# Four seven-product pairs per gate and up unit, with two of their sums made by accumulating transfers

## The chip, the core and the metric

One core of a Trainium2 chip runs the kernel. The metric is the time on the device in microseconds (us), the median of several runs. Five engines work side by side, each through its own queue in order: TensorE (PE) multiplies, VectorE (DVE) and ScalarE (ACT) do elementwise work, GpSimd (POOL) and SyncE (SP) here mostly start transfers. Which instruction stands where in each queue is decided when the program is built, by a scheduler of the library that the kernel is written with; the program cannot change that order while it runs.

## The reference

A decoder layer in float32 on 256 tokens with 16 meta tokens ahead: a SwiGLU block, a mixer (differential attention beside a short convolution, gated and merged), a second SwiGLU block and a norm. What the change touches is the second SwiGLU and the gates of the merge:

```python
def swiglu_ffn(h, w_gu, w_down):
    gate, up = jnp.split(h @ w_gu, 2, axis=-1)
    return (jax.nn.silu(gate) * up) @ w_down
...
        z = jnp.einsum('blnw,nwd->blnd', ys, w_branch[layer])
        gates = jax.nn.sigmoid(h @ w_gate[layer]).reshape(Bsz, L, N_BRANCH, D_MODEL)
        merged = jnp.sum(gates * z, axis=2)
        s = s + merged @ w_out[layer]

        h = rms_norm(s, norm_ffn2[layer])
        s = s + 0.5 * swiglu_ffn(h, ffn2_w_gu[layer], ffn2_w_down[layer])
```

`D_MODEL` is 2048 and `D_FF` 5632. By the end of the mixer only the 256 real tokens are carried on.

## The kernel before, in words

**Split products.** Each float32 operand is split into a high and a low part. ACT casts a weight tile to its high part `wh` (L378), DVE subtracts it from the tile and keeps the rest as `wl` (L379); both lie in rings of three tiles (`W_BUFS`). A product of an activation block and a weight block is then three matmuls into one PSUM bank: high by `wh` (L485), low by `wh` (L486), high by `wl` (L487). Each has 128 rows and 512 columns here.

**Units.** `Mixed`, `linear_mix` and `mixed` compute two outputs of 512 columns for 256 tokens at once: a gate and an up group of the second SwiGLU (10 of its 11 groups; the first is done plainly by `linear_tok`), or the two gates of the merge (4 units). One such call is called a unit here. It runs over 8 pairs of 128-row chunks, and `KINDS` says how each pair is multiplied. A "D" pair takes the 2 x 2 x 2 block product as it stands: 8 products, in 2 weight tiles of 4 products each. An "S" pair uses seven products of sums of blocks (a scheme of Strassen's kind): 4 weight tiles with 1, 2, 2 and 2 products. The eight accumulators are called "1" to "7" and "x". `KINDS = "DDDSDSDS"` has three S pairs (3, 5 and 7, counted from 0), so a unit has 5 x 24 + 3 x 21 = 183 matmuls.

**Sums.** The four sums of activation blocks of an S pair are made once (`pair`, kept in tiles `sp`). Its four weight sums are made for each unit from the loaded tile `st`, on DVE, when the pair is loaded, one pair ahead: L512 makes two of them (the first and third) in one instruction of 128x1024, L513 and L514 the other two (128x512 each). The four lie in one tile `tt`, taken from the same ring of five (`ST_BUFS`) as the loads.

**Order.** `parts` splits a tile, and `step` keeps the tile's products back until two further tiles have been split (`AHEAD = 2`). When a product's accumulator is complete, `done` evicts it: "1" by an ACT copy into `cup` (L553), "x" by an ACT copy into `u2x` (L548), the others by DVE additions, of which "2" into `cgate` is the first (L558). In an S pair the accumulators end in the order 3, 1, 2, 6, 4, 5, 7. The result of a unit is activated, turned by PE (`mt_ps`, L591) and split (L595, L596) during pair 2 of the next unit. All weights come through SP's queue (L508 here), two transfers of 512 KB for each pair.

**Around the units.** The second SwiGLU runs in thirds of 4, 4 and 3 groups, each followed by a down projection (`linear_tok`, tile names `pd`). POOL has almost nothing to do: a few small loads at the start and, near the end, two loads of 512 KB for the last norm (`gfin`, L986).

Of the kernel before, what the change touches and what calls it, by code (L numbers as in the profile page):

```python
# [29 lines left out]
LAM_INIT = 0.8 - 0.6 * math.exp(-0.3 * 0)  # L30
KB = 2
W_BUFS = 3
ST_BUFS = 5
LB = 2
N_ACT = 27
EVICT_AT = 1
WARM = 6
WARM_PREP = 5
HOLD = 3
LATER_AT = (4, 6)  # L40
KINDS = "DDDSDSDS"
AHEAD = 2


# [1 line left out]
def decoder_layer(ctx: ExitStack, tc: tile.TileContext, t, out):  # L46
# [2 lines left out]
    const = ctx.enter_context(tc.tile_pool(name="const", bufs=1))  # L49
    wpool = ctx.enter_context(tc.tile_pool(name="w", bufs=W_BUFS))  # L50
    apool = ctx.enter_context(tc.tile_pool(name="a", bufs=N_ACT))
    tmp = ctx.enter_context(tc.tile_pool(name="tmp", bufs=2))
    psum = ctx.enter_context(tc.tile_pool(name="ps", bufs=8, space=bass.MemoryType.PSUM))

# [259 lines left out]
    def linear_tok(ops, chunks, k0, name, evict, side_at=(5, 9, 13), hold=0, after=None):  # L314
# [46 lines left out]
        for b, c in enumerate(chunks):  # L361
# [9 lines left out]
            wh, wl = parts(st[:, b % 2])  # L371
            step(lambda b=b, wh=wh, wl=wl: use(b, wh, wl))

    def parts(src, n=2):
# [3 lines left out]
        nc.scalar.copy(out=wh, in_=src)  # L378
        nc.vector.tensor_sub(wl, src, wh.bitcast(F32))  # L379
        return wh, wl  # L380

    ng = F // GW
# [44 lines left out]
    class Mixed:  # L427

        def __init__(self, norm, g0):
            self.act, self.sums = Act("hn", 0, SEQ), {}
            self.norm, self.g0 = norm, g0

        def renorm(self, p):
# [10 lines left out]
        def pair(self, p, f):  # L446

            tl = apool.tile([P, 2, 2, SEQ], F32R, tag="act", name=f"hn{p}")
            self.act.tiles.append(tl)
            nc.scalar.copy(out=tl[:, :, 0, :], in_=f)  # L450
            nc.vector.tensor_sub(tl[:, :, 1, :], f, tl[:, :, 0, :].bitcast(F32))
            if KINDS[p] == "S":
                a11, a12, a21, a22 = (f[:, c, i * P : (i + 1) * P] for i in range(2) for c in range(2))
                q = tmp.tile([P, 4, P], F32, tag="sc", name="sums")
                nc.vector.tensor_sub(q[:, 0, :], a21, a22)
                nc.vector.tensor_sub(q[:, 1, :], q[:, 0, :], a11)
                nc.vector.tensor_sub(q[:, 2, :], a11, a21)
                nc.vector.tensor_add(q[:, 3, :], a12, q[:, 1, :])
                sp = apool.tile([P, 4, 2, P], F32R, tag="act", name=f"sp{p}")
                nc.scalar.copy(out=sp[:, :, 0, :], in_=q)  # L460
                nc.vector.tensor_sub(sp[:, :, 1, :], q, sp[:, :, 0, :].bitcast(F32))
                self.sums[p] = [[sp[:, k, lo, :] for lo in range(2)] for k in range(4)]
# [4 lines left out]
    def linear_mix(a, w, cols, name, done):  # L467

        nd, ns = KINDS.count("D"), KINDS.count("S")
        left = {k: 2 * nd * (k in "234x") + ns * (k != "x") for k in "1234567x"}
        ps = {}

        def product(k, left_op, wh, wl):
            first = k not in ps  # L480
            if first:
                ps[k] = bank(name + k)
            left[k] -= 1
            hi, lo = left_op
            nc.tensor.matmul(ps[k], hi, wh, start=first, stop=False)  # L485
            nc.tensor.matmul(ps[k], lo, wh, start=False, stop=False)  # L486
            nc.tensor.matmul(ps[k], hi, wl, start=False, stop=left[k] == 0)  # L487
            if left[k] == 0:
                done(k, ps[k])

        def use(p, n, products):

            for k, left_op, wh, wl in products:
                product(k, left_op, wh, wl)
            if p == 2 and later:
                later.pop(0)()
            if n == (1 if KINDS[p] == "D" else 3):
                if p == 0:
                    flush()
                if side:  # L500
                    side.pop(0)()

        def load(p):

            st = wpool.tile([P, 2, 2, GW], F32, tag="st", bufs=ST_BUFS, name="st")
            rows = w[2 * p * P : (2 * p + 2) * P, :].rearrange("(c p) f -> p c f", p=P)
            for q in range(2):
                nc.sync.dma_start(out=st[:, :, q, :], in_=rows[:, :, cols[q] : cols[q] + GW])  # L508
            if KINDS[p] == "D":
# [3 lines left out]
            nc.vector.tensor_add(tt[:, 2, :], tt[:, 0, :], st[:, 1, 1, :])  # L513
            nc.vector.tensor_add(tt[:, 3, :], tt[:, 2, :], st[:, 1, 0, :])  # L514
            return st, tt

        loaded = {0: load(0)}
        for p, kind in enumerate(KINDS):
            st, tt = loaded[p]
# [14 lines left out]
            for n, (src, products) in enumerate(tiles):  # L534
                if n == 1 and p + 1 < len(KINDS):
# [5 lines left out]
    def mixed(a, w, cols, name, end):  # L541

        ev = {}

        def done(k, ps):
            if k == "x":
                ev["u"] = wide([P, 2, GW], "u2x")
                nc.scalar.copy(out=ev["u"][:, 1, :], in_=ps)  # L548
            elif k == "3":
                ev["p3"] = ps  # L550
            elif k == "1":
                ev["e"], ev["g"] = wide([P, 2, GW], "cup"), wide([P, 2, GW], "cgate")
                nc.scalar.copy(out=ev["e"][:, 0, :], in_=ps)  # L553
            if k in "x31":
                return
            up, gt, u = ev["e"], ev["g"], ev["u"]
            if k == "2":
                nc.vector.tensor_add(gt[:, 0, :], ps, up[:, 0, :])  # L558
            elif k == "6":
                nc.vector.tensor_add(u[:, 0, :], ps, up[:, 0, :])  # L560
            elif k == "4":
                nc.vector.tensor_add(gt[:, 1, :], ps, u[:, 0, :])
            elif k == "5":
                nc.vector.tensor_sub(up[:, 0, :], ps, u[:, 0, :])
                nc.vector.tensor_add(up[:, 1, :], up[:, 0, :], u[:, 1, :])
                nc.vector.tensor_add(up[:, 0, :], ev["p3"], up[:, 0, :])
            elif k == "7":
                nc.vector.tensor_add(gt[:, 1, :], ps, gt[:, 1, :])
                nc.vector.tensor_sub(up[:, 1, :], up[:, 1, :], ps)

                pending.append(lambda: end(gt, up))

        linear_mix(a, w, cols, name, done)

    def gate_up_mix(a, w_gu, g, m, gi):


        def end(gt, up):
            nc.scalar.activation(gt, gt, AF.Silu)
            nc.vector.tensor_mul(up, up, gt)  # L580
            for k in range(2):
                later.append(lambda k=k: back(m, 2 * gi + k, up, k))

        mixed(a, w_gu, (g * GW, F + g * GW), "pg", end)

    def back(act, g, mt, k):

# [250 lines left out]
    n0 = NMETA - 2  # L838
    nu = T - n0
    yc = Act("yc", NH, SEQ)  # L840
    hg = Mixed(norm2, G_MIX)
# [122 lines left out]
    hn = Mixed(norm3, G_FFN2)  # L964

    def renorm_after(b):
        if b % 2 and b > 1:
# [74 lines left out]
```

## Time and profile before

| What | us |
|---|---|
| median of 3 runs | 2203.83 (2202.94 to 2204.87) |
| the profiled execution, its own time | 2203.69 |
| its span, from the first to the last instruction | 2201.9 |
| granted TensorE clock, share of full speed | 0.999 |
| the four gate units with their branch products, from | 1117 to about 1375 |
| second SwiGLU, plain group, from about | 1475 to 1521 |
| second SwiGLU, ten units and three down projections | 1521 to about 2190 |

The page gives, for each engine, its busy time, then the costliest groups of instructions with the mean time of one and what ended the idle time before them. A view of windows gives the busy time of each engine between two moments; a timeline gives single instructions with their start, their length and, in brackets, how long the engine sat idle before and what released it. Matmuls are pipelined, so the record of one (0.39 us) is longer than the distance to the next; the distance between two starts is what one costs.

### The profile page before, as it was taken

What the parts mean: (1) busy time and instruction counts of PE and PEld (TensorE: products, weight loads), DVE (VectorE), ACT (ScalarE), POOL (GpSimd) and SP (SyncE); (2) the same over time, 40 slices, a digit from 0 to 9 for tenths busy, and PEclk for the clock granted to TensorE, in tenths of its full rate; (3) what the DMA queues carried; (4) which work ended last, traced back from release to release, by engine and by line L of the source; (5) the groups of instructions that cost most, each with busy time, mean ns of one, the idle gap of its engine ahead of it and who ended that gap; (6) DMA issues with size and microseconds to landing.
All of it is one profiled execution on the core that took longest, in us unless ns stands there. A gap on an engine that the chain in (4) does not pass through costs nothing.

```text
span 2201.9 us, 33218 instructions
## 1 busy us (share of the span) xinstructions
PE 2186.8 (99%) x13534; PEld 1973.6 (90%) x13534; DVE 1467.6 (67%) x1904; ACT 1041.3 (47%) x1301; POOL 6.4 (0%) x17
## 2 busy tenths in 40 slices
PE   9999999999999999999999999999999999999998
PEld 9999999999999999898988888888888888888886
DVE  7555554445555565667897777678886688856985
ACT  6343433334343443444555455455554455534554
POOL 0000000000000000000000000000000000000000
PEclk9999999999999999999999999999999999999999
DMA  8555555555555555444545666554566566665562
GB/s 273 173 173 173 174 177 178 179 173 173 172 173 176 178 179 176 154 148 140 173 153 192 210 203 217 175 189 147 196 216 207 164 200 202 220 209 182 182 227 96
DMA packets 192393, 401.96 MB, mean 183 GB/s; under 512 B 8692, under 2 KB 8880, under 8 KB 192240
## 3 DMA queue, kind: packets, MB, share of 16 engines
q1 hardware_dynamic: 191232, 397.97, 55.0%
q8 instruction: 105, 1.72, 0.3%
q0 software_dynamic: 544, 1.21, 0.2%
q10 hardware_dynamic: 464, 0.66, 0.1%
q14 instruction: 48, 0.39, 0.1%
HBM read 397.71 MB, written 2.10 MB: 182 GB/s over the span
## 4 chain that ended last, share of the span: by engine, by line
PE 97%; DVE 1%; ACT 1%; DMA 0%; issue 0%; SPq 0%; DVEq 0%; ACTq 0%
PE pg L487 5%; PE pg L485 5%; PE pg L486 5%; PE pu L289 4%; PE pd L289 4%; PE pd L287 4%; PE pu L287 4%; PE pu L288 4%; PE pd L288 4%; PE pg L289 4%; PE pg L287 4%; PE pg L288 4%; PE pd L329 4%; PE pd L327 4%; PE pd L328 4%; PE o L285 3%
## 5 line engine op out<-in xcount | busy, mean ns | idle before, releaser
L276 DVE TENSOR_TENSOR wl<-st,wh 128x1024 fp32r<-128x1024 f32 x392 | 479.2, 1225 | 453.0 <-ACT wh L275 452.5
L275 ACT CAST wh<-st 128x1024 fp32r<-128x1024 f32 x392 | 411.0, 1049 | 609.8 <-PE pd L288 147.0
L378 ACT CAST wh<-st 128x1024 fp32r<-128x1024 f32 (+1 forms) x360 | 358.6, 1003 | 379.6 <-PE pd L328 129.8
L379 DVE TENSOR_TENSOR wl<-st,wh 128x1024 fp32r<-128x1024 f32 (+1 forms) x360 | 415.6, 1161 | 139.4 <-ACT wh L378 138.7
L287 PE MATMUL pg<-h,wh 128*128 128x272 f32 x704 | 203.0, 289 | 0.4 <-ACT wh L275 0.3
L287 PE MATMUL pu<-h,wh 128*128 128x272 f32 x704 | 203.2, 289 | 0.0
L289 PE MATMUL pu<-h,wl 128*128 128x272 f32 x704 | 203.0, 288 | 0.0
L289 PE MATMUL pd<-m,wl 128*128 128x272 f32 x704 | 203.0, 288 | 0.0
L287 PE MATMUL pd<-m,wh 128*128 128x272 f32 x704 | 203.0, 288 | 0.0
L288 PE MATMUL pd<-m,wh 128*128 128x272 f32 x704 | 202.4, 288 | 0.0
L288 PE MATMUL pu<-h,wh 128*128 128x272 f32 x704 | 202.4, 288 | 0.0
L288 PE MATMUL pg<-h,wh 128*128 128x272 f32 x704 | 201.8, 287 | 0.0
L289 PE MATMUL pg<-h,wl 128*128 128x272 f32 x704 | 200.6, 289 | 0.9 <-DVE wl L276 0.9
L485 PE MATMUL pg<-wh,hn 128*128 128x512 f32 x390 | 152.7, 392 | 0.0
L487 PE MATMUL pg<-wl,hn 128*128 128x512 f32 x390 | 151.9, 392 | 0.2 <-DVE wl L379 0.2
L486 PE MATMUL pg<-wh,hn 128*128 128x512 f32 x390 | 152.0, 390 | 0.0
L327 PE MATMUL pd<-wh,m 128*128 128x512 f32 x352 | 137.6, 391 | 0.0
L328 PE MATMUL pd<-wh,m 128*128 128x512 f32 x352 | 137.1, 389 | 0.0
L329 PE MATMUL pd<-wl,m 128*128 128x512 f32 x352 | 137.0, 390 | 0.0
L379 DVE TENSOR_TENSOR wl<-tt,wh 128x1024 fp32r<-128x1024 f32 x84 | 101.3, 1223 | 52.3 <-ACT wh L378 42.4
L287 PEld LDWEIGHTS pg<-h,wh 128*128 128x128 f32 x704 | 132.3, 188 | 1.0 <-ACT wh L275 1.0
L288 PEld LDWEIGHTS pg<-h,wh 128*128 128x128 f32 x704 | 132.8, 189 | 0.0
(303 smaller groups left out, 4728.5 us busy)
## 6 DMA issues: line engine op xcount, KB each, us to landing
st<-in_ffn_w_gu_dram SPq DMA_DIRECT2D x184, 512.0 KB, 4.7
st<-in_ffn_w_down_dram SPq DMA_DIRECT2D x88, 1024.0 KB, 5.2
st<-in_ffn_w_gu_dram SPq DMA_DIRECT2D x84, 1024.0 KB, 5.1
st<-in_w_in_dram SPq DMA_DIRECT2D x48, 1024.0 KB, 5.1
st<-in_w_gate_dram SPq DMA_DIRECT2D x64, 512.0 KB, 4.6
st<-in_w_branch_dram SPq DMA_DIRECT2D x32, 512.0 KB, 5.0
st<-in_w_out_dram SPq DMA_DIRECT2D x16, 1024.0 KB, 5.0
xin<-in_x_dram SPq DMA_DIRECT2D x8, 256.0 KB, 8.5
```

Of the source, the lines that this page charges most:

```text
L275: nc.scalar.copy(out=wh[:, :m, :], in_=sw)
L276: nc.vector.tensor_sub(wl[:, :m, :], sw, wh[:, :m, :].bitcast(F32))
L287: nc.tensor.matmul(a, wh[:, i, f], act.part(c, 0, t0, t1), start=first, stop=False)
L288: nc.tensor.matmul(a, wh[:, i, f], act.part(c, 1, t0, t1), start=False, stop=False)
L289: nc.tensor.matmul(a, wl[:, i, f], act.part(c, 0, t0, t1), start=False, stop=last)
L327: nc.tensor.matmul(ps, hi, wh[:, q, :], start=first, stop=False)
L328: nc.tensor.matmul(ps, lo, wh[:, q, :], start=False, stop=False)
L378: nc.scalar.copy(out=wh, in_=src)
L379: nc.vector.tensor_sub(wl, src, wh.bitcast(F32))
L485: nc.tensor.matmul(ps[k], hi, wh, start=first, stop=False)
L486: nc.tensor.matmul(ps[k], lo, wh, start=False, stop=False)
L487: nc.tensor.matmul(ps[k], hi, wl, start=False, stop=left[k] == 0)
```

## The change

- FFN2's units get their own kinds, `"DDDSSDSS"`: four S pairs (3, 4, 6, 7) and four D pairs, 4 x 24 + 4 x 21 = 180 matmuls in a unit. The gates keep `"DDDSDSDS"`.
- The four weight sums no longer lie in one tile of the load ring. `t13` holds the first and third, `t24` the other two, each 128 x 1024; `t24`, and in the gates `t13` as well, comes from a ring of two tiles called `tt`. The load ring has four tiles instead of five.
- In FFN2, `t13` is made by POOL: one transfer brings two weight blocks from memory, and a second adds two more to them (`accum_op`). Its tiles come from a ring of three, `aux`. Both transfers are asked for up to four pairs ahead. In the gates DVE still makes `t13` when the pair is loaded.
- `t24` is made on DVE by `sum24`, right behind the first split of its own pair, and is held there by `issue_after`.
- The activation ring has 24 tiles instead of 27; the activation sums of the gates lie in `aux` until FFN2 uses it, and those of FFN2 in the activation ring.

```diff
-ST_BUFS = 5
+ST_BUFS = 4
 LB = 2
-N_ACT = 27
+N_ACT = 24
+N_AUX = 3
...
-KINDS = "DDDSDSDS"
+KINDS_GATES = "DDDSDSDS"
+KINDS_FFN2 = "DDDSSDSS"
...
+    aux = ctx.enter_context(tc.tile_pool(name="aux", bufs=N_AUX))
...
         nc.scalar.copy(out=wh, in_=src)
-        nc.vector.tensor_sub(wl, src, wh.bitcast(F32))
+        split_last[0] = nc.vector.tensor_sub(wl, src, wh.bitcast(F32)).ins
...
-                sp = apool.tile([P, 4, 2, P], F32R, tag="act", name=f"sp{p}")
+                sp = (aux if self.in_aux else apool).tile([P, 4, 2, P], F32R, tag="act", name=f"sp{p}")
...
-            if KINDS[p] == "D":
-                return st, None
-            tt = wpool.tile([P, 4, GW], F32, tag="st", bufs=ST_BUFS, name="tt")
-            nc.vector.tensor_add(tt[:, 0:2, :], st[:, 0, :, :], st.rearrange("p c q f -> p q c f")[:, 1, :, :])
-            nc.vector.tensor_add(tt[:, 2, :], tt[:, 0, :], st[:, 1, 1, :])
-            nc.vector.tensor_add(tt[:, 3, :], tt[:, 2, :], st[:, 1, 0, :])
-            return st, tt
+            if kinds[p] == "D":
+                return st, None, None
+            if fetch:
+                t13 = fetched.pop(p)
+            else:
+                t13 = wpool.tile([P, 2, GW], F32, tag="tt", bufs=2, name="t13")
+                nc.vector.tensor_add(t13, st[:, 0, :, :], st.rearrange("p c q f -> p q c f")[:, 1, :, :])
+            return st, t13, wpool.tile([P, 2, GW], F32, tag="tt", bufs=2, name="t24")
+
+        def sum24(st, t13, t24):
+            nc.vector.tensor_add(t24[:, 0, :], t13[:, 0, :], st[:, 1, 1, :])
+            nc.vector.tensor_add(t24[:, 1, :], t24[:, 0, :], st[:, 1, 0, :])
+
+        fetched = {}
+
+        def prefetch(p):
+            t13 = fetched[p] = aux.tile([P, 2, GW], F32, tag="act", name="t13")
+            rows = w[2 * p * P : (2 * p + 2) * P, :].rearrange("(c p) (q f) -> p c q f", p=P, q=2)
+            fs = slice(cols[0], cols[0] + GW)
+            nc.gpsimd.dma_start(out=t13, in_=rows[:, 0, :, fs])
+            nc.gpsimd.dma_start(out=t13, in_=rows[:, :, 1, fs], accum_op=ALU.add)
...
+            if fetch:
+                for k in range(0 if p == 0 else p + 4, min(p + 5, len(kinds))):
+                    if kinds[k] == "S":
+                        prefetch(k)
+            st, t13, t24 = loaded[p]
...
-                    (tt[:, 2:4, :], (("6", s2, 0), ("4", a22, 1))),
-                    (tt[:, 0:2, :], (("5", s1, 0), ("7", s3, 1))),
+                    (t24, (("6", s2, 0), ("4", a22, 1))),
+                    (t13, (("5", s1, 0), ("7", s3, 1))),
...
                 wh, wl = parts(src, src.shape[1])
+                if kind == "S" and n == 0:
+
+                    with tc.issue_after(split_last[0]):
+                        sum24(st, t13, t24)
```

The scheduler also places the rows around the sums anew. Two places of the seventh unit show it. Lines in the changed program are numbered anew: the cast L378 is now L383, the split L379 is L384, the copies L548 and L553 are L577 and L582, the additions L513 and L514 are L526 and L527, L558 is L587 and L596 is L625. Behind each name stands the number of its buffer.

ACT, around pair 7, before. `wh<-tt` are the casts of the third and fourth weight tile of pair 7, `cup<-pg1` is the eviction of accumulator "1".

```order
L378 CAST wh_18087<-st_18070 128x512
L378 CAST wh_18103<-st_18070 128x1024
L378 CAST wh_18121<-tt_18073 128x1024
L548 COPY u2x_18119<-pgx_17847 128x512
L378 CAST wh_18128<-tt_18073 128x1024
L553 COPY cup_18135<-pg1_17971 128x512
L378 CAST wh_18144<-st_18142 128x1024
```

The same place now; `t24_18205` and `t13_18042` are the third and fourth weight tile of pair 7.

```order
L383 CAST wh_18224<-t24_18173 128x1024
L577 COPY u2x_18222<-pgx_17978 128x512
L383 CAST wh_18231<-t13_18003 128x1024
L383 CAST wh_18241<-st_18202 128x512
L383 CAST wh_18253<-st_18202 128x1024
L582 COPY cup_18277<-pg1_18108 128x512
L383 CAST wh_18263<-t24_18205 128x1024
L383 CAST wh_18270<-t13_18042 128x1024
L383 CAST wh_18286<-st_18284 128x1024
```

The eviction of "1", which stood behind both casts of pair 7's sums, now stands ahead of both.

DVE, from pair 4 (a D pair) to the end of pair 5, before. L512 to L514 make the sums of pair 5.

```order
L379 TENSOR_TENSOR wl_17979<-st_17934,wh_17978 128x1024
L512 TENSOR_TENSOR tt_17992<-st_17989 128x1024
L379 TENSOR_TENSOR wl_17997<-st_17934,wh_17996 128x1024
L513 TENSOR_TENSOR tt_17992<-tt_17992,st_17989 128x512
L379 TENSOR_TENSOR wl_18009<-st_17989,wh_18008 128x512
L514 TENSOR_TENSOR tt_17992<-tt_17992,st_17989 128x512
L379 TENSOR_TENSOR wl_18028<-st_17989,wh_18027 128x1024
L379 TENSOR_TENSOR wl_18044<-tt_17992,wh_18043 128x1024
L379 TENSOR_TENSOR wl_18051<-tt_17992,wh_18050 128x1024
```

DVE now, from pair 3 to the end of pair 4, both S pairs. `m4` and `m5` belong to the unit before; `t24_18025` and `t13_17926` are pair 3's, `t24_18073` and `t13_17929` pair 4's.

```order
L625 TENSOR_TENSOR m4_16843<-mt_ps_18063,m4_16843 128x2x256
L384 TENSOR_TENSOR wl_18098<-t24_18025,wh_18097 128x1024
L625 TENSOR_TENSOR m5_16844<-mt_ps_18090,m5_16844 128x2x256
L384 TENSOR_TENSOR wl_18105<-t13_17926,wh_18104 128x1024
L384 TENSOR_TENSOR wl_18116<-st_18070,wh_18115 128x512
L526 TENSOR_TENSOR t24_18073<-t13_17929,st_18070 128x512
L384 TENSOR_TENSOR wl_18132<-st_18070,wh_18131 128x1024
L527 TENSOR_TENSOR t24_18073<-t24_18073,st_18070 128x512
L384 TENSOR_TENSOR wl_18144<-t24_18073,wh_18143 128x1024
L384 TENSOR_TENSOR wl_18151<-t13_17929,wh_18150 128x1024
```

The second half of `t24` now stands behind the split of the pair's second tile, directly ahead of the split that needs it.

More of the change, by code (lines that the diff above doesn't have):

```diff
@@ L372, in linear_tok @@
             step(lambda b=b, wh=wh, wl=wl: use(b, wh, wl))
+    split_last = [None]
     def parts(src, n=2):
@@ L427, in decoder_layer, with __init__ @@
     class Mixed:
-        def __init__(self, norm, g0):
-            self.act, self.sums = Act("hn", 0, SEQ), {}
+        def __init__(self, kinds, norm, g0, in_aux):
+            self.kinds, self.act, self.sums, self.in_aux = kinds, Act("hn", 0, SEQ), {}, in_aux
             self.norm, self.g0 = norm, g0
@@ L451, in pair @@
             nc.vector.tensor_sub(tl[:, :, 1, :], f, tl[:, :, 0, :].bitcast(F32))
-            if KINDS[p] == "S":
+            if self.kinds[p] == "S":
                 a11, a12, a21, a22 = (f[:, c, i * P : (i + 1) * P] for i in range(2) for c in range(2))
@@ L465, in block, with linear_mix @@
             return [self.act.part(c, lo, i * P, (i + 1) * P) for lo in range(2)]
-    def linear_mix(a, w, cols, name, done):
-        nd, ns = KINDS.count("D"), KINDS.count("S")
+    def linear_mix(a, w, cols, name, done, fetch):
+        kinds = a.kinds
+        nd, ns = kinds.count("D"), kinds.count("S")
         left = {k: 2 * nd * (k in "234x") + ns * (k != "x") for k in "1234567x"}
@@ L496, in use @@
                 later.pop(0)()
-            if n == (1 if KINDS[p] == "D" else 3):
+            if n == (1 if kinds[p] == "D" else 3):
                 if p == 0:
@@ L508, in load @@
                 nc.sync.dma_start(out=st[:, :, q, :], in_=rows[:, :, cols[q] : cols[q] + GW])
-            if KINDS[p] == "D":
-                return st, None
-            tt = wpool.tile([P, 4, GW], F32, tag="st", bufs=ST_BUFS, name="tt")
-            nc.vector.tensor_add(tt[:, 0:2, :], st[:, 0, :, :], st.rearrange("p c q f -> p q c f")[:, 1, :, :])
-            nc.vector.tensor_add(tt[:, 2, :], tt[:, 0, :], st[:, 1, 1, :])
-            nc.vector.tensor_add(tt[:, 3, :], tt[:, 2, :], st[:, 1, 0, :])
-            return st, tt
-        loaded = {0: load(0)}
-        for p, kind in enumerate(KINDS):
-            st, tt = loaded[p]
+            if kinds[p] == "D":
[16 more added lines that the diff above has]
+            nc.gpsimd.dma_start(out=t13, in_=rows[:, :, 1, fs], accum_op=ALU.add)
+        loaded = {0: load(0)}
+        for p, kind in enumerate(kinds):
+            if fetch:
[3 more added lines that the diff above has]
+            st, t13, t24 = loaded[p]
             (a11, a21), (a12, a22) = ([a.block(2 * p + c, i) for i in range(2)] for c in range(2))
@@ L530, in linear_mix, with mixed @@
                     (st[:, :, 0, :], (("1", a11, 0), ("2", a12, 1))),
-                    (tt[:, 2:4, :], (("6", s2, 0), ("4", a22, 1))),
-                    (tt[:, 0:2, :], (("5", s1, 0), ("7", s3, 1))),
+                    (t24, (("6", s2, 0), ("4", a22, 1))),
+                    (t13, (("5", s1, 0), ("7", s3, 1))),
                 ]
             for n, (src, products) in enumerate(tiles):
-                if n == 1 and p + 1 < len(KINDS):
+                if n == 1 and p + 1 < len(kinds):
                     loaded[p + 1] = load(p + 1)
                 wh, wl = parts(src, src.shape[1])
+                if kind == "S" and n == 0:
+                    with tc.issue_after(split_last[0]):
+                        sum24(st, t13, t24)
                 products = [(k, left_op, wh[:, j, :], wl[:, j, :]) for k, left_op, j in products]
                 step(lambda p=p, n=n, products=products: use(p, n, products))
-    def mixed(a, w, cols, name, end):
+    def mixed(a, w, cols, name, end, fetch=False):
         ev = {}
@@ L571, in done @@
                 pending.append(lambda: end(gt, up))
-        linear_mix(a, w, cols, name, done)
+        linear_mix(a, w, cols, name, done, fetch)
     def gate_up_mix(a, w_gu, g, m, gi):
@@ L582, in end @@
                 later.append(lambda k=k: back(m, 2 * gi + k, up, k))
-        mixed(a, w_gu, (g * GW, F + g * GW), "pg", end)
+        mixed(a, w_gu, (g * GW, F + g * GW), "pg", end, fetch=True)
     def back(act, g, mt, k):
@@ L840, in decoder_layer @@
     yc = Act("yc", NH, SEQ)
-    hg = Mixed(norm2, G_MIX)
+    hg = Mixed(KINDS_GATES, norm2, G_MIX, True)
     for g in range(2):
@@ L963, in decoder_layer @@
     w_gu, w_down = t["ffn2_w_gu"][0], t["ffn2_w_down"][0]
-    hn = Mixed(norm3, G_FFN2)
+    hn = Mixed(KINDS_FFN2, norm3, G_FFN2, False)
     def renorm_after(b):
```

## The prediction

> **What bounds the kernel now.** I read the page first, then the chain of waits, then windows over single FFN2 units, then the timelines of PE, ACT and DVE inside one unit.
>
> ```profile
> PE 2186.8 (99%) x13534; PEld 1973.6 (90%) x13534; DVE 1467.6 (67%) x1904; ACT 1041.3 (47%) x1301; POOL 6.4 (0%) x17
> PE 97%; DVE 1%; ACT 1%; DMA 0%; issue 0%; SPq 0%; DVEq 0%; ACTq 0%
> ```
>
> The first line is busy time, the second the chain that ended last. PE is the bound, nearly without a gap. Windows over three units in a row (start:end, then busy time and count for PE, PEld, DVE, ACT, POOL, granted clock, DMA share, GB/s):
>
> ```profile
> 1794.25:1836.99 42.74, 42.74 (x193) 34.84 (x192) 37.96 (x44) 24.25 (x28) 0.00 (x0) 1.00 0.61 197
> 1836.99:1879.72 42.73, 42.73 (x193) 34.84 (x192) 37.97 (x44) 24.28 (x28) 0.00 (x0) 1.00 0.61 197
> 1879.72:1922.45 42.73, 42.73 (x194) 34.84 (x192) 36.91 (x41) 24.69 (x28) 0.00 (x0) 1.00 0.69 227
> ```
>
> A unit takes 42.73 us and PE is busy throughout. DVE's 37.96 us is the warning: 89% of the same window, on the engine that must finish every split before PE can use it. What one matmul costs is the distance between starts:
>
> ```profile
> 1809.11 0.39 PE L487 MATMUL pg<-wl,hn 128*128 128x512 f32 x1
> ...
> 1817.75 0.39 PE L486 MATMUL pgx<-wh,hn 128*128 128x512 f32 x1
> 1817.97 0.39 PE L487 MATMUL pgx<-wl,hn 128*128 128x512 f32 x1
> 1818.20 0.39 PE L485 MATMUL pg<-wh,sp 128*128 128x512 f32 x1
> ...
> 1823.50 0.39 PE L485 MATMUL pg<-wh,hn 128*128 128x512 f32 x1
> 1823.75 0.50 PE L487 MATMUL pg<-wl,hn 128*128 128x512 f32 x1
> ```
>
> From 1809.11 to 1818.20 lie 40 matmuls: 0.227 us each. Pair 7 of this unit starts at 1818.20. The next unit's first low-part product at 1823.75 comes 0.02 us late and then runs 0.11 us long: a small wait for its split, about 0.1 us in each unit. So PE is not far ahead of its suppliers even now.
>
> **What is removed.** An S pair has 21 matmuls, a D pair 24. One more S pair in each of 10 units takes 30 matmuls away, 10 x 3 x 0.227 = 6.8 us. If nothing else came in PE's way the profiled execution's 2203.69 us would become 2196.9.
>
> **DVE's amount** hardly changes. Its rows over pairs 5 to 7:
>
> ```profile
> 1813.63 1.22 DVE L379 TENSOR_TENSOR wl<-st,wh 128x1024 fp32r<-128x1024 f32 x1
> 1814.76 0.69 DVE L513 TENSOR_TENSOR tt<-tt,st 128x512 f32<-128x512 f32 x1
> 1815.36 0.69 DVE L379 TENSOR_TENSOR wl<-st,wh 128x512 fp32r<-128x512 f32 x1
> 1815.96 0.69 DVE L514 TENSOR_TENSOR tt<-tt,st 128x512 f32<-128x512 f32 x1
> 1816.57 1.22 DVE L379 TENSOR_TENSOR wl<-st,wh 128x1024 fp32r<-128x1024 f32 x1
> 1819.30 1.23 DVE L379 TENSOR_TENSOR wl<-tt,wh 128x1024 fp32r<-128x1024 f32 x1 [1.51 <-ACT wh L378]
> 1820.73 1.23 DVE L379 TENSOR_TENSOR wl<-tt,wh 128x1024 fp32r<-128x1024 f32 x1 [0.21 <-ACT wh L378]
> 1821.88 0.69 DVE L558 TENSOR_TENSOR cgate<-pg,cup 128x512 f32<-128x512 f32 x1
> 1822.48 1.22 DVE L379 TENSOR_TENSOR wl<-st,wh 128x1024 fp32r<-128x1024 f32 x1
> ```
>
> By starts, 128x1024 costs 1.13 us and 128x512 0.60. A D pair has two splits, 2.27 us; an S pair had 3 x 1.13 + 0.60 for splits and 1.13 + 2 x 0.60 for sums, 6.33, and has 5.20 without L512. Before: 5 x 2.27 + 3 x 6.33 = 30.3; now 4 x 2.27 + 4 x 5.20 = 29.9 us a unit. The amount is not the matter; the place is. In these rows L513 and L514 are through by 1816.6, while PE is still in pair 6. Bound behind its own pair's first split, and with two S pairs in a row, `t24` becomes late. Two waits follow, from ACT's rows:
>
> ```profile
> 1815.45 1.05 ACT L378 CAST wh<-st 128x1024 fp32r<-128x1024 f32 x1 [2.10 <-DVE tt L513]
> 1818.22 1.05 ACT L378 CAST wh<-tt 128x1024 fp32r<-128x1024 f32 x1 [1.71 <-PE pgx L486]
> 1819.17 0.58 ACT L548 COPY u2x<-pgx 128x512 f32<-128x512 f32 x1
> 1819.65 1.05 ACT L378 CAST wh<-tt 128x1024 fp32r<-128x1024 f32 x1
> 1820.61 0.58 ACT L553 COPY cup<-pg 128x512 f32<-128x512 f32 x1
> 1821.08 2.98 ACT L378 CAST wh<-st 128x1024 fp32r<-128x1024 f32 x3
> ```
>
> The cast at 1818.22 waited for a matmul that started at 1817.75 and ended at 1818.14, so from PE to ACT it takes 0.08 us; a cast takes 1.05 us, and a copy holds ACT for 0.47.
>
> **First wait, pair 7.** Before, the copy of "1" into `cup` stood behind both casts of pair 7's sums. The order now has it ahead of them, and ACT runs in order: the cast of `t24` must wait for accumulator "1" of the same pair. PE's order there is three matmuls of "3", two of "1", one of "2", the last of "1", two more of "2", then "6", which needs the cast. Counted from pair 7's start, "1" is issued last at 6 x 0.227 = 1.36 and ends at 1.75; the copy starts at 1.83, frees ACT at 2.30, the cast ends at 3.35, and PE goes on at 3.4. It was ready at 9 x 0.227 = 2.04. That is 1.35 us in which PE has nothing to do. Behind the cast PE has six high-part matmuls before it needs a low part, 1.36 us, so DVE's split (1.23 us, begun as the cast ends) is just in time, and DVE's evictions come as late behind PE as before. No queue can overtake this; only if PE wrote "1" sooner would it shrink.
>
> **Second wait, pair 4.** `wh` has three buffers, so the cast of pair 4's second tile (ACT) waits until PE is through with the high part of pair 3's third tile: 14 matmuls into pair 3, at 13 x 0.227 + 0.39 + 0.08 = 3.42 us from its start. The cast ends at 4.47; DVE splits from 4.5, adds the second half of `t24` from 5.65 to 6.34 (it stands directly behind), ACT casts it by 7.4, PE goes on at 7.5. PE wants that tile at (21 + 9) x 0.227 = 6.81. Late by 0.65 us if DVE is free at 4.5. It hardly is: `m5` waits for the transposes that end pair 2, so the split of pair 3's `t13` begins about 2.4, and behind it stand 1.13 + 0.60 + 0.60 of other rows, so the second tile's split begins at 4.75. The whole is then about 0.9 us late. I take 0.9; 0.65 is the lower end. Pair 6 follows a D pair, and there this chain has 5.4 us of D products to hide behind: no wait, and likewise none in the gates, where every S pair follows a D pair.
>
> **Sum.** Per unit -0.68 + 1.35 + 0.9, less the 0.1 us wait that the old order had at this place: +1.45 us. Ten units: +14.5; 2203.7 + 14.5 = 2218.
>
> **Other edits.**
>
> ```profile
> st<-in_ffn_w_gu_dram SPq DMA_DIRECT2D x184, 512.0 KB, 4.7
> PE pg L289 <- DVE wl L276: 0.9, 2, 0.6
> ```
>
> The load ring loses a tile, but the sums leave it too, and a load lands in 4.7 us against four pairs of some 5 us each between request and use. At the start the fifth weight load moves behind the four last loads of x and waits for DVE; the second row says that PE waits for splits in that block 0.9 us in all (2 times, 0.6 at most), so I put this at 0, within 1. The activation ring's three tiles are those of the gates' sums; a wait for one would show in the gates or the plain group: 0, up to 1 us. POOL had nothing in FFN2 that could be held up.
>
> **Transfers.** The added ones are eight of 512 KB in a unit, half of them accumulating.
>
> ```profile
> q1 hardware_dynamic: 191232, 397.97, 55.0%
> gfin<-in_norm_final_dram POOLq DMA_DIRECT2D x2, 512.0 KB, 5.9
> 1959.09 0.56 POOL L986 DMA_DIRECT2D gfin<-in_norm_final_dram  x1 [1952.85 <-PE pd L329]
> 15.00:20.00 5.00, 5.00 (x43) 5.00 (x42) 4.92 (x12) 4.03 (x9) 0.00 (x0) 1.00 1.05 386
> ```
>
> A plain transfer of this size from POOL lands in 5.9 us beside SP's stream. The tightest one is pair 7's: its tile is pair 3's, free when pair 3's last split is done, and wanted some 16 us later (pairs 4 to 6, less DVE's lead). Two transfers one after the other take 11.8 us if an accumulating one costs what a plain one does: hidden. It may take up to 10 us before DVE waits. No row shows an accumulating transfer, so its cost is bounded by 5.9 us below and, reading the target back as well as the source, by twice the bytes above.
>
> In bytes: SP's 16 transfers are 8.39 MB a unit, the added eight 4.19 MB. 197 GB/s filled 0.61 of the engines, so full share is 323 GB/s; 12.58 MB in 44.2 us are 285 GB/s, a share of 0.88. It fits.
>
> The Trainium skill, "Collectives: The Full Stack" (section "The bandwidth ceiling: the fold count and why AG ≠ RS ≠ AR"), holds that an add inside a transfer costs no arithmetic time but needs two source reads on one ring, and halves the rate. No row here shows it; it speaks for the upper bound and for the third case below.
>
> **Rivals.**
>
> *Only pair 7 waits.* DVE catches up in pair 4 and only the copy holds PE: -0.68 + 1.35 - 0.1 = +0.57 a unit, 2209. For it: DVE idles 1.5 us at 1819.30. Against: the chain through ACT, DVE and ACT again is longer than the seven matmuls it must hide behind.
>
> *Thirty matmuls go and nothing waits: faster, 2197.* This needs both the copy and the sum to run earlier than the order lets them. It decides if the chain in pair 7 is under 0.7 us longer than PE's work, so that the wait no longer eats the 0.68 us; I count 1.35. Against it is that each step is a row above.
>
> *Transfers become the bound.* If the accumulating ones fill the engines twice, a unit moves 14.7 MB in engine time: 14.7 / 323 GB/s = 45.4 us instead of 42.73, which gives 2203.7 + 10 x 2.7 = 2231, and more if pair 7's tile misses its 16 us, by 10 us in all for each us of lateness. For it: 0.61 is already used. Against: the window at 15 us moved 386 GB/s, at which 14.7 MB take 38 us.
>
> *The change doesn't do what it says:* the third sums could still be made on DVE, or the order differ from the diff; the order shows neither.
>
> **Chances.** Forecast (both waits, transfers hidden) 0.58; only pair 7 0.14; transfers 0.18; nothing waits 0.10. Changes within 0.2% (4.4 us, about what a measurement of this kernel can tell from none) lie between 2199.3 and 2208.1: 0.06, taken from the second and last case. Faster 0.08, slower 0.86. The forecast's own range, from 0.65 to 1.2 us for the second wait and 0.2 us either way for the first, is 2214 to 2223. To hold 8 in 10 the range reaches down to just under the pair-7 case and up past the transfer case by some lateness: 2206 to 2238.
>
> **What would show it.** Right: units of about 44.2 us; in each a PE gap of 1.2 to 1.5 us before a high-part matmul on `t24`, released by ACT's cast, the copy to `cup` directly ahead of that cast; a second gap of 0.6 to 1 us half a unit earlier; DVE's sums not waiting for transfers; DMA share near 0.9; gate units as long as before. Wrong: gaps released by a transfer, DVE idle ahead of L526, landings over 10 us, units of 42.1 us, or lost time outside the ten units.

## The result and the profile after

| | before | after |
|---|---|---|
| median of the runs, us | 2203.39 (2201.94 to 2204.87, 4 runs) | 2219.45 (2219.04 to 2220.02, 4 runs) |
| span of the profiled execution, us | 2201.9 | 2217.7 |
| mean granted clock | 0.999 | 0.998 |

The changed kernel is slower by 0.73%: the ratio to the kernel before is 1.0073, 95% interval 1.0061 to 1.0086.

The page of the changed kernel, busy time and the chain that ended last. PE has 30 matmuls fewer, and its share of the chain fell from 97% to 95%; ACT and DVE, with 1% each before, have 2% each. That is the first sign of waiting on them.

```profile
PE 2185.2 (99%) x13504; PEld 1964.2 (89%) x13504; DVE 1468.5 (66%) x1919; ACT 1053.8 (48%) x1322; POOL 82.5 (4%) x97
PE 95%; DVE 2%; ACT 2%; issue 1%; DMA 0%; SPq 0%; ACTq 0%; DVEq 0%
```

Windows over two FFN2 units of the changed kernel (start:end, length, then busy time and count for PE, PEld, DVE, ACT and POOL, granted clock, DMA share, GB/s):

```profile
1766.64:1811.17 44.53, 42.81 (x189) 33.95 (x189) 37.97 (x44) 25.40 (x30) 7.56 (x8) 1.00 0.95 283
1811.17:1855.70 44.53, 42.80 (x188) 33.95 (x189) 37.99 (x44) 25.39 (x30) 7.60 (x8) 1.00 0.95 283
```

A unit takes 44.53 us instead of 42.73, and PE is busy in 42.81 of them, where before it was busy in all. DVE's amount is what it was (37.97).

PE's waits, summed over the execution (us in total, times, longest):

```profile
PE pg L492 <- ACT wh L383: 17.2, 20, 1.2
```

Twenty waits in ten units, all for ACT's cast. In the units the view lists none for a transfer, and none for DVE directly. The timeline of PE shows both in one unit (start, duration, line, and in brackets the idle time before it with what ended it):

```profile
1854.74 0.40 PE L494 MATMUL pg<-wl,hn 128*128 128x512 f32 x1
1855.70 0.50 PE L492 MATMUL pg<-wh,sp 128*128 128x512 f32 x1 [0.56 <-ACT wh L383]
1856.03 0.39 PE L493 MATMUL pg<-wh,sp 128*128 128x512 f32 x1
...
1868.89 0.39 PE L492 MATMUL pg<-wh,sp 128*128 128x512 f32 x1
...
1870.76 0.39 PE L494 MATMUL pg<-wl,hn 128*128 128x512 f32 x1
1872.31 0.50 PE L492 MATMUL pg<-wh,sp 128*128 128x512 f32 x1 [1.17 <-ACT wh L383]
1872.65 0.40 PE L493 MATMUL pg<-wh,sp 128*128 128x512 f32 x1
```

The row at 1868.89 is the first of pair 7. The idle time in brackets begins where the matmul before has drained. What is lost is read from start to start: 0.96 us instead of 0.227 in pair 4, 1.55 instead of 0.227 in pair 7, so 0.73 and 1.32 us; the matmul behind each gap comes another 0.1 us late (0.33 and 0.34 us after it instead of 0.227). ACT at the same places:

```profile
1851.36 1.06 ACT L383 CAST wh<-st 128x1024 fp32r<-128x1024 f32 x1 [0.75 <-PE pg L493]
1854.60 2.00 ACT L383 CAST wh<-t 128x1024 fp32r<-128x1024 f32 x2 [2.19 <-DVE t L527]
...
1867.41 1.05 ACT L383 CAST wh<-st 128x1024 fp32r<-128x1024 f32 x1 [0.36 <-PE pg L493]
1870.73 0.59 ACT L582 COPY cup<-pg 128x512 f32<-128x512 f32 x1 [2.26 <-PE pg L494]
1871.21 2.00 ACT L383 CAST wh<-t 128x1024 fp32r<-128x1024 f32 x2
```

And DVE ahead of them:

```profile
1852.67 1.22 DVE L384 TENSOR_TENSOR wl<-st,wh 128x1024 fp32r<-128x1024 f32 x1
1853.81 0.68 DVE L527 TENSOR_TENSOR t<-t,st 128x512 f32<-128x512 f32 x1
...
1868.92 1.22 DVE L384 TENSOR_TENSOR wl<-st,wh 128x1024 fp32r<-128x1024 f32 x1
1870.06 0.68 DVE L527 TENSOR_TENSOR t<-t,st 128x512 f32<-128x512 f32 x1
```

In pair 4 the chain is plain: the split starts at 1852.67, the second half of `t24` (L527) follows and ends at 1854.49, the cast runs from 1854.60, PE goes on at 1855.70. In pair 7 two things end close together. The copy of "1" into `cup` (L582) holds ACT until 1871.21, as forecast; but L527 ends only at 1870.74, when that copy has just begun. Without the copy the cast could have started at about 1870.8, 0.4 us sooner, and no more. The prediction had put all of this wait on the copy.

### The profile page after: what moved, and what is told of

Read it like the earlier page. It is cut to its first block, busy times and chain, and to the rows that moved or that the text cites. A ratio compares the mean times of both kernels' runs of the same rounds, so it can differ in the third digit from the quotient of the medians.

```text
span 2217.7 us, 33326 instructions
## 1 busy us (share of the span) xinstructions
PE 2185.2 (99%) x13504; PEld 1964.2 (89%) x13504; DVE 1468.5 (66%) x1919; ACT 1053.8 (48%) x1322; POOL 82.5 (4%) x97
## 3 DMA queue, kind: packets, MB, share of 16 engines
q0 software_dynamic: 17184, 43.16, 8.4%
## 4 chain that ended last, share of the span: by engine, by line
PE 95%; DVE 2%; ACT 2%; issue 1%; DMA 0%; SPq 0%; ACTq 0%; DVEq 0%
PE pg L492 5%; PE pg L494 5%; PE pg L493 5%; PE pu L292 4%; PE pd L292 4%; PE pu L290 4%; PE pd L290 4%; PE pd L291 4%; PE pu L291 4%; PE pg L292 4%; PE pg L290 4%; PE pg L291 4%; PE pd L330 4%; PE pd L332 4%; PE pd L331 4%; PE o L288 3%
## 5 line engine op out<-in xcount | busy, mean ns | idle before, releaser
L383 ACT CAST wh<-st 128x1024 fp32r<-128x1024 f32 (+1 forms) x360 | 352.2, 991 | 356.9 <-PE pd L331 132.6
L384 DVE TENSOR_TENSOR wl<-st,wh 128x1024 fp32r<-128x1024 f32 (+1 forms) x360 | 407.9, 1144 | 150.0 <-ACT wh L383 148.5
L384 DVE TENSOR_TENSOR wl<-t,wh 128x1024 fp32r<-128x1024 f32 x104 | 124.9, 1222 | 63.7 <-ACT wh L383 48.0
L383 ACT CAST wh<-t 128x1024 fp32r<-128x1024 f32 x104 | 106.6, 1050 | 76.4 <-DVE t L527 21.7
L492 PE MATMUL pg<-wh,hn 128*128 128x512 f32 x360 | 141.1, 392 | 0.0
L493 PE MATMUL pg<-wh,hn 128*128 128x512 f32 x360 | 140.5, 390 | 0.0
L494 PE MATMUL pg<-wl,hn 128*128 128x512 f32 x360 | 138.1, 394 | 0.0
L290 PEld LDWEIGHTS pg<-h,wh 128*128 128x128 f32 x704 | 132.3, 188 | 1.4 <-ACT wh L278 1.4
```

What stands on the lines that cost most here:

```text
L290: nc.tensor.matmul(a, wh[:, i, f], act.part(c, 0, t0, t1), start=first, stop=False)
L384: split_last[0] = nc.vector.tensor_sub(wl, src, wh.bitcast(F32)).ins
```

## The experiments

Two theories stood against each other. **Order**: binding the sums to their place behind the pair's first split makes `t24` late in the two pairs that follow another seven-product pair, and nothing else costs time. **Transfers**: the accumulating transfers, or the short ring that they fill, cost the time, by load or by lateness. Every edit below is to the changed kernel, and line numbers are those of the run they stand with. The ratios are to the kernel before, run again beside each set of experiments (2204.37 to 2204.39 us). Where a unit's length is given "from copy to copy", it is the distance between the ACT copies of "1" of two units in a row.

**1. The sums free of their place.**

```diff
-                    with tc.issue_after(split_last[0]):
-                        sum24(st, t13, t24)
+                    sum24(st, t13, t24)
```

> The sums of t24 stay where they are in the program, but nothing holds them behind the split; the order then has the eviction of accumulator 1 behind both casts of pair 7, and pair 4's and pair 7's sums one pair earlier. Theory A (the order of ACT and DVE makes both waits): the casts of t24 no longer hold PE, so those 20 waits are gone. But pair 7's transfers are now wanted about 11 us after pair 3's tile is free, and in the changed kernel's trace the pair of them took 13 to 15 us, so DVE should idle some 3 us ahead of L526 in each unit and PE some 2: units near 44 us, 2210 to 2222, gaps at pair 6 instead of pairs 4 and 7. Theory B (the load of the transfers on the DMA engines as such is the cost): PE waits for casts as before, 2219.

Measured: 2224.55 us (2218.40 to 2227.39, 4 runs), ratio 1.0087, interval 1.0069 to 1.0104; the median lies above the 2210 to 2222 expected. First PE's waits and DVE's for a transfer, then one such wait and the transfers that it belongs to:

```profile
PE pg L494 <- DVE wl L384: 18.7, 10, 3.3
...
DVE t L526 <- DMA t<-in_ffn_w_gu_dram: 38.5, 10, 5.3
```

```profile
1853.88 0.74 POOL L535 DMA_DIRECT2D t<-in_ffn_w_gu_dram  x1 [7.92 <-DVE wl L384]
1858.40 1.18 POOL L536 DMA_DIRECT2D t<-in_ffn_w_gu_dram  x1 [3.78 <-DMA t<-in_ffn_w_gu_dram]
1865.21 0.69 DVE L526 TENSOR_TENSOR t<-t,st 128x512 f32<-128x512 f32 x1 [3.41 <-DMA t<-in_ffn_w_gu_dram]
```

The twenty waits for ACT are gone, and one new wait a unit has come. Free of its place, L526 stands so early in DVE's order that the transfers of pair 7 have not landed: the tile is handed over at 1853.9 and the sum wants it some 8 us later, with DVE idle for 3.4 us and every split behind it late.

The ten waits of PE are uneven, 0.9 to 3.3 us, and the mean granted clock is 0.994 to 0.996 against 0.998 in the changed kernel. In the trace it is low only behind the longest waits:

```profile
1913.11 0.80 PE L494 MATMUL pg<-wl,hn 128*128 128x512 f32 x1 [2.88 <-DVE wl L384]
1913.70 0.63 PE L492 MATMUL pg<-wh,hn 128*128 128x512 f32 x1
1914.13 0.63 PE L493 MATMUL pg<-wh,hn 128*128 128x512 f32 x1
```

Behind the three longest waits (2.88, 3.05 and 3.30 us) matmuls start 0.43 us apart instead of 0.227, for 5 to 12 matmuls, and the granted clock of these stretches is 0.50 to 0.57; behind the other seven, of up to 2.47 us, it is 1.00. So the lower clock goes with the long waits and is counted as part of their cost. Whether this kernel is slower than the changed one stays open, because the intervals of the two ratios overlap; no gain shows.

With a ring of three tiles the bound order costs two waits on ACT, the free order one on a transfer. A fourth tile tells what of this is the ring's.

**2. Three pairs by transfers.** The pattern of before, with the transfers and the bound sums kept.

```diff
-KINDS_FFN2 = "DDDSSDSS"
+KINDS_FFN2 = "DDDSDSDS"
```

> FFN2 goes back to three S pairs, DDDSDSDS; the transfers and the bound sums stay, so 6 transfers a unit instead of 8. Theory A: no two S pairs are neighbours, the order has the eviction of 1 behind the casts, so no waits: units of 42.7 us, 2203 (2201 to 2206). Theory B: three quarters of the loss stays, about 2.5 x 0.75 us a unit over 42.7: 2220.

Measured: 2202.10 us (2201.36 to 2204.43, 10 runs), ratio 0.9990, interval 0.9980 to 0.9999. PE has no wait in FFN2, and the unit, here from copy to copy, is 42.73 us, as in the kernel before:

```profile
1818.89:1861.62 42.73, 42.73 (x193) 34.84 (x192) 35.10 (x39) 24.28 (x28) 5.79 (x6) 1.00 0.89 267
```

Bound sums and accumulating transfers cost nothing where each S pair follows a D pair, at a DMA share of 0.89. The loss needs two S pairs in a row.

**3. The second transfer plain.** It overwrites the first one's data instead of adding to it, so this kernel leaves out the addition of the two weight blocks.

```diff
-            nc.gpsimd.dma_start(out=t13, in_=rows[:, :, 1, fs], accum_op=ALU.add)
+            nc.gpsimd.dma_start(out=t13, in_=rows[:, :, 1, fs])
```

> The second transfer of each sum overwrites instead of adding: the same number of bytes from memory, the same order. It leaves out the addition in t13, so products 5, 7 and the sums built on it are of other blocks. Theory A: the same time within 2 us, 2219, the same 20 waits. Theory B, with a cost of the accumulating: faster by 5 us or more, and the second transfer lands clearly sooner than the 7.4 us (median) it took; by bytes read twice I would expect 5 to 6 us.

Measured: 2219.25 us (one run). PE's waits and one unit's window:

```profile
PE pg L492 <- ACT wh L383: 17.2, 20, 1.2
...
1811.17:1855.70 44.53, 42.81 (x189) 33.99 (x189) 37.99 (x44) 25.40 (x30) 5.79 (x8) 1.00 0.85 284
```

The DMA share falls from 0.95 to 0.85. The waits are the same, and from copy to copy the unit is shorter by no more than 0.03 us (44.50 to 44.53). What the accumulation costs the transfer engines is wholly hidden here.

**4. Free sums, four tiles.** Experiment 1 with a fourth tile in the ring; a small constant moved to another pool makes the room for it.

```diff
-N_AUX = 3
+N_AUX = 4
-    lamv = const.tile([P, 4, HD], F32, name="lamv")
+    lamv = tmp.tile([P, 4, HD], F32, tag="aB", name="lamv")
-                    with tc.issue_after(split_last[0]):
-                        sum24(st, t13, t24)
+                    sum24(st, t13, t24)
```

> As the unbound kernel, with a fourth tile in the ring of the transfers (one small tile of the start, lamv, moves into a ring of later use to make room). The transfers of pair 7 no longer wait for pair 3's tile of the same unit. Theory A: nothing is left to wait for, units of 42.1 us, 2197 (2195 to 2200), faster than both kernels. Theory B: the eight transfers a unit are still there, at 12.6 MB in 42.1 us, 300 GB/s; if the DMA engines are the bound units stay at 44 us or more, 2215 to 2225.

Measured: 2195.92 us (2195.66 to 2196.44, 5 runs), ratio 0.9960, interval 0.9946 to 0.9974: faster than both kernels. Two units in a row:

```profile
1790.51:1832.70 42.19, 42.19 (x190) 34.26 (x189) 37.96 (x44) 25.92 (x30) 7.45 (x8) 1.00 0.98 300
1832.70:1874.90 42.20, 42.20 (x191) 34.24 (x189) 37.66 (x44) 25.91 (x30) 6.83 (x8) 1.00 0.98 297
```

PE is busy throughout, beside transfers at a share of 0.98. ACT's order has changed with the sums: the copy of "1" now stands behind both casts of pair 7.

**5. Four tiles, sums bound.** The ring's share alone; the small constant moves as in experiment 4, here and in the next two. The order of ACT and DVE is that of the changed kernel, row for row.

```diff
-N_AUX = 3
+N_AUX = 4
```

> The changed kernel with a ring of four tiles, the sums still bound; the order is the same on every engine. If the order makes the two waits: 2219, the same two waits a unit (17 us in all before L492), DMA share higher. If the ring of three tiles was part of the loss: at or near 2196.

Measured: 2219.64 us (2219.13 to 2219.84, 4 runs), ratio 1.0068, interval 1.0053 to 1.0084.

```profile
PE pg L492 <- ACT wh L383: 17.2, 20, 1.2
```

The same waits to the tenth. So the fourth tile is no gain by itself; it is what the free order needs. The 23.7 us between this kernel and that of experiment 4 are the price of the bind, 2.37 us a unit.

**6 and 7. One pair freed at a time.** Four tiles; in the first only pair 7's sum is free, in the second only pair 4's.

```diff
-                    with tc.issue_after(split_last[0]):
+                    with ExitStack() if kinds is KINDS_FFN2 and p == 7 else tc.issue_after(split_last[0]):
```

> Four tiles; in FFN2 only pair 7's sum is free of its place, pairs 3, 4 and 6 stay bound. The order then has the sum one pair earlier and the copy behind both casts, on both counts as in the kernel of 2195.9. If the two waits are separate and as measured: pair 7's goes, 10 x 1.42 us: about 2205, with 10 waits of about 0.73 us left. If curing one wait only moves it to another place: above 2210.

> Four tiles; in FFN2 only pair 4's sum is free, pairs 3, 6 and 7 stay bound; ACT's order is that of the changed kernel. If the two waits are separate: pair 4's goes, 10 x 0.8 to 0.95 us: about 2210 to 2211.5, with 10 waits of about 1.2 to 1.3 us left. If PE's earlier arrival lengthens the wait of pair 7 or of the D pair between: 2214 to 2219.

Measured: pair 7 free 2205.01 us (2204.84 to 2205.61, 10 runs), ratio 1.0003, interval 0.9993 to 1.0012; pair 4 free 2209.11 us (2208.25 to 2210.99, 10 runs), ratio 1.0023, interval 1.0014 to 1.0032, a little under the 2210 to 2211.5 expected. PE's waits with pair 7 free, and the wait that is left in one unit:

```profile
PE pg L492 <- ACT wh L383: 5.6, 10, 0.6
...
1805.71 0.50 PE L492 MATMUL pg<-wh,sp 128*128 128x512 f32 x1 [0.56 <-ACT wh L383]
```

And with pair 4 free:

```profile
PE pg L492 <- ACT wh L383: 11.6, 10, 1.2
...
1824.64 0.50 PE L492 MATMUL pg<-wh,sp 128*128 128x512 f32 x1 [1.16 <-ACT wh L383]
```

5.6 and 11.6 are the 17.2 of the bound kernel, cut in two. Against experiment 4, the wait of pair 4 costs 2205.01 - 2195.92 = 9.1 us, or 0.91 a unit, and that of pair 7 costs 13.2 us, or 1.32. Together 22.3 of the 23.7; the two waits are separate, and curing one does not lengthen the other.

**8. The copy of "1" behind the casts.** Three tiles, sums bound; only ACT's order in pair 7 is changed.

```diff
-        nc.scalar.copy(out=wh, in_=src)
+        cast_last[0] = nc.scalar.copy(out=wh, in_=src).ins
...
-                nc.scalar.copy(out=ev["e"][:, 0, :], in_=ps)
+                with tc.issue_after(cast_last[0]):
+                    nc.scalar.copy(out=ev["e"][:, 0, :], in_=ps)
```

> The sums stay bound; only ACT's copy of accumulator 1 into cup is held behind the last cast of pair 7. If, as the prediction counted, the whole wait of pair 7 (1.32 us measured) is the copy ahead of the cast, it goes: about 2206. If the sum itself is late there too (its second half ends at 1870.74 in the changed kernel, when the copy has just started), the cast starts at 1870.8 instead of 1871.2 and PE gains only some 0.45 us a unit: about 2215, with a wait of about 0.85 us left, released by the cast, whose own releaser is then the sum of L527. If the evictions that the late copy holds up matter: no gain, 2219 or more.

Measured: 2216.69 us (2215.72 to 2217.51, 5 runs), ratio 1.0055, interval 1.0043 to 1.0068. Pair 7 in the timelines of DVE, ACT and PE:

```profile
1824.51 0.68 DVE L527 TENSOR_TENSOR t<-t,st 128x512 f32<-128x512 f32 x1
...
1825.30 2.00 ACT L383 CAST wh<-t 128x1024 fp32r<-128x1024 f32 x2 [2.37 <-DVE t L527]
1827.20 0.58 ACT L583 COPY cup<-pg 128x512 f32<-128x512 f32 x1
...
1825.21 0.40 PE L494 MATMUL pg<-wl,hn 128*128 128x512 f32 x1
1826.40 0.50 PE L492 MATMUL pg<-wh,sp 128*128 128x512 f32 x1 [0.79 <-ACT wh L383]
```

The copy is out of the way, and the cast's releaser is now the sum of L527, ended at 1825.19. From start to start the gap is 1.19 us instead of 1.55. The kernel gains 2.8 us, 0.28 a unit, where the prediction's account would give back 13. The copy was only the last 0.3 to 0.4 us of that wait; behind it stood the same late sum as in pair 4.

**9. No transfers.** The kernel of experiment 4 with DVE making the first two sums as well, into the same ring.

```diff
-        mixed(a, w_gu, (g * GW, F + g * GW), "pg", end, fetch=True)
+        mixed(a, w_gu, (g * GW, F + g * GW), "pg", end)
...
-                t13 = wpool.tile([P, 2, GW], F32, tag="tt", bufs=2, name="t13")
+                t13 = (aux if kinds is KINDS_FFN2 else wpool).tile([P, 2, GW], F32, tag="act" if kinds is KINDS_FFN2 else "tt", bufs=N_AUX if kinds is KINDS_FFN2 else 2, name="t13")
```

The second edit holds in FFN2 alone; other callers keep the tile that they had.

> The kernel of 2195.9 (four tiles, no sum bound) without the accumulating transfers: DVE makes the first two sums of each seven-product pair itself, into the same ring. Queue POOL is then empty in FFN2 and the DMA share falls from 0.98 to about 0.6. DVE gets 4 x 1.13 = 4.5 us a unit more than its 38.0, so 42.5 in a unit of 42.2. If the transfers are what pays for the fourth pair: DVE becomes the bound, units of 43 to 45 us with PE waiting for DVE's splits, 2203 to 2225. If they only look useful and DVE still keeps ahead: 2196 to 2199.

Measured: 2198.41 us (2198.05 to 2200.58, 8 runs), ratio 0.9974, interval 0.9963 to 0.9984. That lies outside the first expectation (2203 to 2225) and inside the second. Two units, from copy to copy, and PE's waits there in all ten:

```profile
1774.33:1816.57 42.24, 42.24 (x191) 34.67 (x190) 41.87 (x48) 25.83 (x30) 0.00 (x0) 1.00 0.62 200
1816.57:1859.57 43.00, 42.26 (x189) 33.90 (x188) 41.95 (x48) 25.66 (x31) 0.00 (x0) 1.00 0.60 195
...
PE pg L492 <- ACT wh L383: 2.2, 3, 0.7
```

DVE is busy in 41.9 of 42.2 us and PE still waits only three times in ten units; a unit with such a wait takes 43.0 us. With the order free, the 80 transfers are worth 2.5 us (2198.41 against 2195.92; the two sets of runs do not overlap), and these three waits are 2.2 of it. Of the 8.5 us by which the kernel of experiment 4 is faster than the one before, 6.0 come without the transfers.

## Why the prediction was right

**The time.** 2218 was predicted and 2219.45 measured, on the side to which 0.86 was given, in the range and in the forecast's own range of 2214 to 2223. The unit was put at 44.2 us and took 44.53, which is 1.80 us more than before where 1.45 was forecast. Ten units would make 18.0 us, and the kernel lost 16.1: around the units it became shorter. The distance between two copies of "1" with a down projection between them grew by 1.50 us (129.98 to 131.48), and the gates became a little shorter (below). That the total comes nearer to the forecast than the unit does is luck.

**The 30 matmuls.** The prediction had 2196.9 for a kernel in which nothing waits, and another 1 us less with the old wait of 0.1 us a unit gone. The kernel of experiment 4, in whose units the view lists no wait of PE, took 2195.92, so the sum holds; its two terms do not. From copy to copy the unit is shorter by 0.54 us (42.73 to 42.19), not by 0.78, and the old wait is still there at another place: a low-part product at 1800.00 comes 0.30 us behind the matmul before it and the next 0.33 behind that, instead of 0.227. Ten units give 5.4 us of the 7.7 between the two profiled executions (2203.69 and 2196.01), the gates about 0.6; where the rest lies was not separated. The agreement to the microsecond is luck.

**Pair 4.** Put at 0.9, with 0.65 as the lower end; experiment 6, with only this wait left, measures 0.91 by whole times and 0.89 from copy to copy (43.08 against 42.19). The chain runs as written: from the split to PE's next start the prediction had 2.95 us (4.75 to 7.7), the trace has 3.03 (1852.67 to 1855.70).

**Pair 7: the size is right, and one of two causes was missed.** Put at 1.35; experiment 7 measures 1.32 by whole times and 1.24 from copy to copy (43.43 against 42.19). Counted from the pair's start at 1868.89 the copy frees ACT after 2.32 us and PE goes on after 3.42, where the prediction had 2.30 and 3.4, so the chain that ended last is the one forecast. The step that failed is "the cast of `t24` must wait for accumulator "1"" as the reason for the whole. The prediction applied the chain of the second wait to pair 4 and pair 6 and not to pair 7, which like pair 4 follows another S pair and so has the same late L527. Two causes with ends 0.47 us apart (1870.74 and 1871.21) covered each other; experiment 8 takes the later one away and gains 0.28 us a unit. Nor is it so that the wait would shrink only "if PE wrote "1" sooner", once the order may change: with pair 7's sum free (experiment 6) the sum stands earlier and the copy behind both casts, and the wait is gone. That run takes both causes away at once. A copy ahead of the cast with an early sum was not run, so that the copy alone would then cost the whole 1.32 us is argued from the timeline only.

**The small rest.** The measured bind costs 2.37 us a unit where the two waits were put at 2.25. The two waits by themselves make 2.23 (0.91 and 1.32), so 0.14 a unit is left over; from copy to copy it is 2.34 less 2.13, or 0.21. Its place was not looked for.

**The gates** were forecast to stay as long as before, and nearly do: the four copies of "1" in their units span 194.1 us before and 193.4 after, 0.2 us less a unit.

```profile
L553 ACT COPY cup<-g x4: 584/584/592, 1164.4 to 1358.5; 128x512 f32<-128x512 f32 x4
```

```profile
L582 ACT COPY cup<-g x4: 584/586/587, 1164.7 to 1358.1; 128x512 f32<-128x512 f32 x4
```

**Transfers.** Hidden, as forecast, and the case in which they are the bound is refuted twice: removing the accumulation changes nothing (experiment 3), and in experiment 4 PE has no wait in its units beside a share of 0.98. The forecast share of 0.88 was too low because it counted the accumulating transfers as plain ones. At the same rate (283 and 284 GB/s) the share is 0.95 with them and 0.85 without: 0.10 x 44.53 = 4.5 us of the engines' time in a unit for four transfers. By bytes four plain ones are a sixth of 0.85 x 44.53, or 6.3 us; an accumulating one thus holds the engines 1.7 times as long as a plain one. That is within the bounds of one and two of the prediction. The Trainium skill, "Collectives: The Full Stack" (section "The bandwidth ceiling: the fold count and why AG ≠ RS ≠ AR"), says of a ReduceScatter between cores that its add needs two source reads and that it so runs at half the rate of a plain copy. The 1.7 measured here, for a transfer within one core, is below that two, and it cost the kernel no time that shows (2219.25 us without the addition, 2219.45 with it).

**What the prediction left out.** It weighed whether the transfers of pair 7 land in time only for the bound order. In the free order the sum comes earlier, and a ring of three tiles is too short for it (experiment 1). The bind costs 2.37 us a unit, but with three tiles taking it away brought no gain: the two waits on ACT gave place to one on a transfer.

## What to carry to other kernels

When a wait is explained by the instruction that ended last, work out when the others would have let go as well: the second of two causes sets what removing the first is worth. A producer bound to a place "behind the previous step" is bound to the end of that step's own chain; where two heavy steps follow each other, as S pairs do here, the binding makes it late in the second. A buffer ring and an order are one choice: the fourth tile alone gave nothing, the free order alone showed no gain, and both together took 23.5 us off the changed kernel.

## What the runs showed of the hardware

An accumulating transfer costs more than its bytes. The second transfers (L536) of the changed kernel, with POOL's time at the issue in ns (min/median/max), the time to landing, and the line of their queue:

```profile
L536 POOL DMA_DIRECT2D t<-in_ffn_w_gu_dram x40: 1172/1183/1259, 1344.8 to 2122.8; - x40
...
DMA to landing us min/median/max: 5.5/7.4/12.1
...
q0 software_dynamic: 17184, 43.16, 8.4%
```

And where they are plain (experiment 3):

```profile
L536 POOL DMA_DIRECT2D t<-in_ffn_w_gu_dram x40: 722/722/743, 1345.0 to 2121.4; - x40
...
DMA to landing us min/median/max: 4.1/5.6/8.7
...
q0 software_dynamic: 12064, 43.16, 6.0%
```

A median of 7.4 us to landing instead of 5.6, and 1.18 us of POOL instead of 0.72. The bytes are the same, and the 5120 packets more are 128 for each of the 40 accumulating transfers. The page counts the same 43.16 MB in both, so a share of the engines' time shows this cost and a rate in GB/s does not.

The DMA share of a unit reached 0.98 at 300 GB/s without one wait on PE: a share near 1 is no sign by itself that transfers are late.

PE pays a little beyond a wait: the matmul behind each gap is followed by the next one after 0.33 to 0.34 us instead of 0.227, in pair 4 and in pair 7 alike. Behind the longest waits it pays more: in experiment 1 the matmuls behind waits of 2.88 to 3.30 us start 0.43 us apart, 5 to 12 of them, at a granted clock of 0.50 to 0.57, while behind waits of up to 2.47 us the clock stays at 1.00.
